# A two-layer hybrid trunk on one core: x, B and C of the scan fetched two chunks sooner, and the order of products and scalings in the output projections changed

## The chip, the core and the metric

The kernel runs on one core of one Trainium2 chip. The core has a matmul engine (TensorE, PE in the profile), VectorE (DVE), ScalarE (ACT), GpSimd (POOL) and SyncE (SP), which here only issues transfers. The metric is the device time of one execution in microseconds (us), lower is better. The profile is one execution, recorded by the hardware profiler; "L1555" in it is line 1555 of the kernel before.

## The reference, cut to what matters

```python
SEQ, D_MODEL, D_INNER = 1024, 1024, 2048          # one sequence, float32

def spatial_gating_mixer(h, w_in, ln_w, ln_b, w_s, b_s, w_out):          # layer 0
    z, u, v = split(h @ w_in, 3)                                         # 1024 -> 6144
    v = layernorm(v)                                                     # in 8 chunks of 128 tokens, 8 groups of 256
    mixed = einsum('gts,bcsgd->bctgd', tril(w_s), v) + b_s
    return (u * mixed * silu(z)) @ w_out                                 # 2048 -> 1024

def ssd_mixer(h, ...):                                                   # layer 1 (Mamba-2)
    z, xbc, dt = split(h @ w_in)                                         # 2048 | 4096 | 32 heads
    xbc = silu(causal_depthwise_conv(xbc, K=4));  x, B, C = split(xbc)
    dA_cs = cumsum(softplus(dt + bias) * A)                              # within a chunk of 128
    y = diag(C B^T * decay * dt) x + C (state before the chunk) * exp(dA_cs) + d_skip * x
    g = group_rmsnorm(y * silu(z), norm_w)                               # 8 groups of 256 channels
    return g @ w_out

h = x
for i in (0, 1): h = h + mixer_i(rmsnorm(h, norm_w[i]))
return rmsnorm(h, final_norm_w)
```

## The kernel before

**Matmuls in three.** Each float32 operand is split into a high part (a cast on ScalarE, L111) and a low part (a subtraction on VectorE, L112, or L742 where it is put off), and each product is three matmuls of 512 columns: high by high, high by low, low by high (`mm3`, L134 to L136). A name ending in h is a high part, in l a low part: `xh`, `xl` are those of a block of activations, `wh`, `wl` those of weights.

**Blocks.** The four large projections are computed as 2 x 2 block products with seven block products in place of eight (`Block` for the projections into a layer, `Out` for those out of it: `ao` for layer 0, `bo` for layer 1). In `Out`, A(i, j, c) is quarter c of block (i, j) of the activations (tiles `ya`), and B(k, l, c) that of the weights (tiles `wb`). `product(n)` runs one block product in four quarters; a quarter is 24 matmuls into four PSUM tiles `o[0]` to `o[3]` (four blocks of rows, two k each, three matmuls each). `prep(n, c)` splits the operands of a quarter, one quarter ahead. The order is 1, 7, 2, 6, 4, 5, 3 in `ao` and 1, 2, 7, 6, 4, 5, 3 in `bo`. Product 7 multiplies A(0, 0) + A(1, 0): the sum is made in place, for the first quarters on VectorE (`plus`, L762) and for the others as a DMA that adds (`add`, L759, on GpSimd's queue). In layer 1 each A quarter is loaded from DRAM (`g_d`, written by the scan) and scaled by the group norm's factors (L1766) when `ready` is called; `hook_b(n, c)` says at which quarter of which product the loads, scalings and sums of `bo` are issued. The factors come over DRAM: sums of squares to `ss_d`, back as `sv`, a power on GpSimd, `rs_d`, and back as `rb`.

**The scan.** Layer 1's scan goes over 64 chunks (8 groups of heads x 8 chunks of 128 tokens), n = 8g + c. Groups 0, 1, 3 and 5 are "spilt": their x, B and C after the convolution lie in DRAM (`xbc_d`) and come back 1 MB (four chunks) at a time by `prefetch(g, th, 0)` (L1555, tile `xbc`); `prefetch(g, th, 1)` loads z and the decay factors (`ze`). For the other groups the projection itself is computed during the scan (matmuls into `ab`, called by `project` as a filler between the scan's own matmuls), and its convolution and SiLU (tiles `x`, `bc`) are put into a queue that `drain` empties step by step. Each chunk loads 256 KB of decay inputs (`wl<-cs_d`, L1590) into one of four buffers, four chunks ahead, in pairs. At chunk n the transposes of chunk n + 3 (`pe_a`, L1595 and L1596, into `tp`), the weights (L1619), the diagonal product (`yy`, L1630), the states (`os`) and the gate follow one another. M = 50 is the chunk at which the projections end and product 1 of `bo` becomes the filler.

**The seam.** The last projection block before the scan runs its seven products in the order 1, 2, 6, 5, 7, 4, 3, one unit each. During it a last part of the activations (`f01`, L1378, tile `f`) is loaded again and split (`hh`, `hl`; `rest_a21`), and the last convolutions (`xc`) are put out.

**What sets the order.** The program order of each engine is the order of the calls; nothing reorders them. Tiles come from pools (16 buffers of 1 MB for `ya`, `wb`, `xbc`, `f`; four for `wl` of the scan; four for `xh` and `xl`), and an instruction that writes a tile waits for the last readers of the buffer's former tile. Transfers wait in the queue of the engine that issues them, and a transfer that waits holds up those behind it.

Of the kernel before, what the change touches and what calls it, by code (L numbers as in the profile page):

```python
# [15 lines left out]
P = 128  # L16
# [13 lines left out]
def kernel(  # L30
# [21 lines left out]
    nc = tc.nc  # L52
    x = x[0]
    out = out[0]
# [607 lines left out]
    class Out:  # L662
# [11 lines left out]
        def __init__(self, src, w, scale, res, accs, keep, order):  # L674
            self.src, self.w, self.scale, self.res, self.accs, self.keep = src, w, scale, res, accs, keep
            self.order, self.had, self.late, self.raw = order, set(), [], {}
            self.A, self.B, self.ops, self.acc, self.u, self.ss, self.guess = {}, {}, {}, {}, {}, {}, {}
            self.Y3, self.negs = [], []

        def half(self, th, nb):  # L680

# [110 lines left out]
        def product(self, n, hook=None):  # L792

            if n in (1, 2, 5):
                self.acc[n] = self.accs(n)
            if n == 4:
                t = s8([P, 4, 512], "u")
                self.u["c21"] = [t[:, k, :] for k in range(4)]
                for i in range(4):
                    nc.sync.dma_start(out=t[:, i, :], in_=self.res(4 + i, 0))  # L800
            o = self.acc[n] = self.acc[{7: 1, 6: 1, 4: 1, 3: 5}.get(n, n)]
            more = n not in (1, 2, 5)
            seq = [(m, c) for m in self.order[:6] for c in range(4)]
            now = n != 2 or self.order[1] == 7
            rest = []

            def low():
                while rest:
                    rest.pop(0)()

            for c in range(4):
                self.prep(n, c)
                at = seq.index((n, c)) + 1
                if at < len(seq) and not (n == 1 and c < 2 and self.scale is not None):
                    self.prep(*seq[at], rest)
                self.flush()
                if n == 1:
                    low()
                if hook is not None:
                    hook(n, c)  # L820
                low()
                X, Y = self.ops.pop((n, c))
                for i in range(4):
                    for k in range(2):
                        mm3(o[i], [m[:, k, i * P:(i + 1) * P] for m in X], [m[:, k, :] for m in Y],
                            not more and c == 0 and k == 0, c == 3 and k == 1, more)
                    if c == 3 and i and now:
                        self.post(n, i - 1)
                    if c == 3 and i == 3 and now:
                        self.post(n, i)  # L830
                    if n == (2 if self.order[1] == 7 else 6) and i == 0:
                        self.add(self.row(0, c, 0), self.res(c, 0))
                    if n == 4 and i == 3:
                        self.add(self.row(1, c, 1), self.res(4 + c, 1))
                    if n == 5 and i == 3:
                        self.add(self.row(0, c, 1), self.res(c, 1))
                    if i == 3:
                        for y in self.negs:
                            nc.scalar.mul(y, y, -1.0)
                        self.negs.clear()  # L840
                    yield
# [142 lines left out]
    late = []  # L984

    def finish():

        while late:
            late.pop(0)()
# [319 lines left out]
    xbc_d, todo = {}, []  # L1309
# [154 lines left out]
    def blocks():  # L1464


        ORDER, LAST = (1, 2, 6, 7, 5, 4, 3), (1, 2, 6, 5, 7, 4, 3)
        for g in SPILT:
            xbc_d[g] = dr.tile([P, 2, 4, 512], F32, name=f"xbc_d{g}")
        pairs = SPILT[:2], SPILT[2:]  # L1470
        bs = [zb[1], xbc_block("x", pairs[0]), zb[2], xbc_block("bc", pairs[0]), xbc_block("x", pairs[1]),
              xbc_block("bc", pairs[1]), zb[3]]
        bs[-1].apart = True
        seq = [(k, n) for k in range(len(bs)) for n in (ORDER if k < len(bs) - 1 else LAST)]
        small, turn, a21, done = decays(), [0], rest_a21(), []

        def ahead(at):
            if at < len(seq):
                k, n = seq[at]
                if n not in bs[k].Y:  # L1480
                    bs[k].prep(n)

        def unit(b, n, i):

            turn[0] += 1
            off = late[:]
            late.clear()
            if b is bs[-1]:
                if n in (1, 6):
                    late.append(todo.pop(0)())  # L1490
            elif done and todo and (turn[0] % 2 or len(todo) > 3):
                late.append(todo.pop(0)())
            b.mm(n, i, b is not bs[-1] or n != 5)
            if b is bs[-1] and n == 7:
                b.post(5, i)
                late.append(todo.pop(0)())
            for f in off:
                f()
            if not done and next(small, 0) == 0:
                done.append(True)  # L1500

        for at, (k, n) in enumerate(seq[1:], 1):
            b, nxt = bs[k], bs[k + 1] if k + 1 < len(bs) else None
            ahead(at + 1)
            if n == (2 if k else 7):
                b.fourth()
            if nxt is not None:
                if n == 1 or at == 1:
                    nxt.load(0, 1)
                if n == 6:  # L1510
                    nxt.load(0, 0)
                elif n == 5:
                    nxt.load(1, 0)
                    nxt.sums_b()
                elif n == 4:
                    nxt.load(1, 1)
            elif n == 6:
                next(pj)
            elif n == 5:
                next(a21)  # L1520
            elif n == 4:
                next(pj)
                next(a21)
            elif n == 3:
                next(pj)
                next(a21, None)
            for i in range(b.units):
                unit(b, n, i)
                if i == 0:
                    if nxt is not None and n == 7:  # L1530
                        nxt.sums_a()
                    ahead(at + 2)
        finish()

    with tc.manual_schedule():
# [245 lines left out]
    def hook_b(n, c):  # L1781
# [9 lines left out]
        elif at == (1, 3):  # L1791
            get("a", 0, 1, 2), get("b", 1, 0, 2)
            end["half"][0][1](), end["half"][0][2]()
            for k in (2, 3):
                get("a", 1, 0, k)
            bo.ready(1, 0, 0)
        elif n == 2:
            if c == 0:
                get("a", 0, 1, 3)
# [8 lines left out]
                bo.ready(1, 1, 0)  # L1808
            if c < 2:
                bo.b12_plus(1, c)  # L1810
            if c < 3:
                bo.ready(1, 0, c + 1)
            (bo.plus if c < 2 else bo.add)(bo.a(0, 0, c), bo.a(1, 0, c))
        elif n == 7:
            if c == 0:
                get("a", 1, 1, 3)
            if c < 2:
                bo.ready(1, 1, c + 1)
            if c < 3:
                bo.sums(2, c)  # L1820
        elif n == 6:
            if c == 0:
                bo.ready(1, 1, 3)
                bo.sums(2, 3)
            bo.sums(6, c)
            if c % 2 == 0:
                get("b12", 0, 1, c)
            if c == 0:
                end["fnwb"] = q4([P, D], "fnwb")
                nc.sync.dma_start(out=end["fnwb"], in_=final_norm_w.partition_broadcast(P))  # L1830
            elif c == 3:
                bo.b12_plus(0, 0)
            if c:
                bo.plus(bo.a(1, 0, c - 1), bo.a(1, 1, c - 1))
        elif n == 4:
            if c == 0:
                bo.plus(bo.a(1, 0, 3), bo.a(1, 1, 3))
                bo.b12_plus(0, 1)
            bo.post(2, c)
            if c % 2:  # L1840
                get("b", 1, 1, c - 1)
        elif n == 5:
            bo.prep_last(c)
            if c:
                weigh_left((c - 1) // 2, 2 * ((c - 1) % 2))
            if c == 3:
                bo.prep_unit(0)
# [13 lines left out]
    def scans():  # L1861
# [27 lines left out]
                    scan[g] = Scan(g, nc.gpsimd)  # L1889
                getattr(scan[g], f)(c, *a)  # L1890

        prefetch(0, 0, 0), prefetch(0, 0, 1)
        project(AHEAD // 2 + 1)
        while todo or late:
            convolve()
# [10 lines left out]
        at("decay", 2)  # L1906
        at("pe_a", 2), at("tokens", 2)
        for n, (g, c) in enumerate(chunks):
            if n == M + 3:
                drain(len(queue))  # L1910
            elif n == N - 9:
                for k in range(2):
                    bo.get("a", 0, 0, k)
            elif n == N - 7:
                end["scan"] = scan[G - 1]
                bo.get("b", 0, 0, 0)
# [60 lines left out]
                rs[g - 1][1]()  # L1977
            if c == 1 and g > 1:
                rs[g - 1][2]()
            k = n + 4  # L1980
            if c % 4 < 2 and k < N:
                prefetch(k // 8, k // 4 % 2, c % 4)
            project(want(n + 1))
        sc = scan[G - 1]
        for k in (0, 1):
# [67 lines left out]
```

## Time and profile before

| what | value |
|---|---|
| time, median of 3 runs (lowest to highest) | 1520.2 us (1519.4 to 1528.06) |
| the profiled execution: its time, its span | 1520.27 us, 1518.6 us |
| TensorE busy, mean granted clock | 1463.4 us (96%), 0.992 |
| VectorE, ScalarE, GpSimd busy | 1049.1, 784.2, 402.0 us (69%, 52%, 26%) |
| matmuls of `ao`: first to last | 530.3 to 690.6 us |
| the scan: first transpose, first and last diagonal product | 1007.3, 1019.0, 1353.7 us |
| matmuls of `bo`: first to last | 1339.1 to 1508.3 us |

A span runs from the first to the last instruction; 1.7 us of the execution's time lie around it. In rows of waits stand the engine, the tile that it wanted to write, the line, then what it waited for, and the total in us, the times and the longest. In rows of the timeline stand start and length in us, the engine ("SPq" is SyncE's queue of transfers), the line, the operation, out<-in, and in square brackets the idle time before it and what ended that. "PEclk" is the clock that TensorE was granted, as a share of full speed. Numbers of buffers are left out of names.

### The profile page before, as it was taken

How to read it: one execution, taken by the hardware profiler on the slowest of the kernel's cores; microseconds unless marked ns; L12 is line 12 of the kernel's file. 1: busy time of each engine (PE TensorE's matmuls, PEld its weight loads, DVE VectorE, ACT ScalarE, POOL GpSimd, SP SyncE). 2: the span in 40 equal slices, each digit the busy share in tenths (PEclk: the TensorE clock that was granted, in tenths of full speed). 3: DMA queues.
4: the chain of work that ended last, by engine and by line, in shares of the span. 5: the costliest groups of instructions: out<-in, count | busy, mean ns of one | idle time of the engine just before them, and what ended most of it. 6: DMA issues, size and time to landing. Idle time of an engine off the chain costs nothing. (4 is left out here: it accounts for less than half of the span.)

```text
span 1518.6 us, 21342 instructions
## 1 busy us (share of the span) xinstructions
PE 1463.4 (96%) x7834; PEld 1230.3 (81%) x7834; DVE 1049.1 (69%) x1713; ACT 784.2 (52%) x1256; POOL 402.0 (26%) x451
## 2 busy tenths in 40 slices
PE   6899999999999999999999999998999989999997
PEld 6899988888888888877878888877787878777875
DVE  7966566676666655678657467766677767688876
ACT  6533332232322445556666566565766676756463
POOL 1111110000000023202131313126666676642221
PEclk9999999999999999999999999999999999999999
DMA  5554323322322999948377888776656555589972
GB/s 183 140 169 143 106 89 108 110 105 101 116 87 79 361 247 243 257 133 163 112 174 161 182 169 162 153 235 188 180 145 191 166 181 140 159 264 276 250 162 111
DMA packets 174952, 254.45 MB, mean 168 GB/s; under 512 B 16400, under 2 KB 103168, under 8 KB 171648
## 3 DMA queue, kind: packets, MB, share of 16 engines
q1 hardware_dynamic: 124768, 168.93, 36.0%
q0 software_dynamic: 42448, 70.27, 23.0%
q10 hardware_dynamic: 7632, 13.90, 2.5%
q8 instruction: 62, 1.02, 0.3%
q14 instruction: 42, 0.34, 0.1%
HBM read 186.14 MB, written 51.18 MB: 156 GB/s over the span
## 5 line engine op out<-in xcount | busy, mean ns | idle before, releaser
L134 PE MATMUL acc<-hh,wh 128*128 128x512 f32 x868 | 340.1, 392 | 0.8 <-ACT u L296 0.8
L136 PE MATMUL acc<-hh,wl 128*128 128x512 f32 x868 | 338.5, 390 | 1.9 <-DVE wl L112 1.8
L135 PE MATMUL acc<-hl,wh 128*128 128x512 f32 x868 | 337.8, 389 | 0.0
L112 DVE TENSOR_TENSOR wl<-wr,wh 128x1024 fp32r<-128x1024 f32 (+1 forms) x96 | 114.3, 1192 | 118.7 <-ACT wh L111 118.6
L136 PEld LDWEIGHTS acc<-hh,wl 128*128 128x128 f32 x868 | 162.9, 188 | 37.8 <-DVE wl L112 3.6
L134 PEld LDWEIGHTS acc<-hh,wh 128*128 128x128 f32 x868 | 163.1, 188 | 35.0 <-ACT u L296 1.8
L135 PEld LDWEIGHTS acc<-hl,wh 128*128 128x128 f32 x868 | 163.0, 188 | 33.2
L296 ACT COPY u<-acc 128x512 f32<-128x512 f32 x115 | 66.9, 583 | 197.8 <-PE acc L136 197.7
L111 ACT CAST wh<-wr 128x1024 fp32r<-128x1024 f32 (+1 forms) x112 | 115.2, 1029 | 94.1 <-PE acc L135 56.6
L136 PE MATMUL acc<-wh,hl 128*128 128x256 f32 x448 | 129.2, 288 | 4.4 <-DVE hl L407 4.0
L134 PE MATMUL acc<-wh,hh 128*128 128x256 f32 x448 | 129.6, 289 | 2.4 <-DVE wh L418 1.0
L135 PE MATMUL acc<-wl,hh 128*128 128x256 f32 x448 | 128.6, 287 | 1.3 <-DVE wl L421 1.3
L134 PE MATMUL ab<-hh,wh 128*128 128x512 f32 x288 | 125.0, 434 | 0.8 <-DVE zt L999 0.8
L136 PE MATMUL ab<-hh,wl 128*128 128x512 f32 x288 | 114.2, 397 | 0.0
L135 PE MATMUL ab<-hl,wh 128*128 128x512 f32 x288 | 113.4, 394 | 0.0
L136 PEld LDWEIGHTS acc<-wh,hl 128*128 128x128 f32 x448 | 87.6, 196 | 5.6 <-DVE hl L407 4.7
L134 PEld LDWEIGHTS acc<-wh,hh 128*128 128x128 f32 x448 | 87.7, 196 | 3.4 <-ACT hh L400 1.4
L135 PEld LDWEIGHTS acc<-wl,hh 128*128 128x128 f32 x448 | 87.7, 196 | 1.7 <-DVE wl L421 1.5
L1601 ACT ACTIVATE wl<-wl,tk 128x128 f32<-128x128 f32 x256 | 81.6, 391 | 4.9 <-DMA wl<-cs_d 4.5
L649 POOL DMA_DIRECT2D y_d<-y x8 | 4.4, 549 | 290.6 <-DVE y L646 290.6
L135 PE MATMUL bo<-wl,xh 128*128 128x512 f32 x192 | 75.8, 395 | 5.4 <-DVE wl L112 2.4
L112 DVE TENSOR_TENSOR wl<-t,wh 128x1024 fp32r<-128x1024 f32 (+1 forms) x38 | 45.5, 1196 | 48.3 <-ACT wh L111 48.2
(314 smaller groups left out, 3248.1 us busy)
## 6 DMA issues: line engine op xcount, KB each, us to landing
wr<-in_a_w_in_dram SPq DMA_DIRECT2D x48, 512.0 KB, 3.7
wl<-cs_d SPq DMA_DIRECT2D x64, 256.0 KB, 4.6
wr<-in_b_w_in_dram SPq DMA_DIRECT2D x30, 512.0 KB, 8.4
wb<-in_a_w_out_dram SPq DMA_DIRECT2D x10, 1024.0 KB, 11.8
wb<-in_b_w_out_dram SPq DMA_DIRECT2D x10, 1024.0 KB, 8.9
wr<-in_b_w_in_dram SPq DMA_DIRECT2D x36, 256.0 KB, 6.0
v<-v_d SPq DMA_DIRECT2D x8, 1024.0 KB, 4.7
y_d<-y POOLq DMA_DIRECT2D x8, 1024.0 KB, 5.7
```

The costliest lines, as they stand in the source:

```text
L111: nc.scalar.copy(out=hi, in_=src)
L112: return (eng or nc.vector).tensor_tensor(out=lo, in0=src, in1=hi.bitcast(F32), op=ALU.subtract)
L134: nc.tensor.matmul(out=o, lhsT=l[0], rhs=r[0], start=start, stop=False, **kw)
L135: nc.tensor.matmul(out=o, lhsT=l[0], rhs=r[1], start=False, stop=False, **kw)
L136: nc.tensor.matmul(out=o, lhsT=l[1], rhs=r[0], start=False, stop=stop, **kw)
L296: nc.scalar.copy(out=self.u[n][:, i], in_=a)
L649: store = lambda: nc.gpsimd.dma_start(out=y_d[-1], in_=y)
L1601: nc.scalar.activation(wl[:, j, :], wl[:, j, :], AF.Relu, scale=-1.0, bias=tokc(2, c, self.g)[:, j:j + 1])
```

## The change

1. *Scan.* `prefetch` of part 0 (the 1 MB of x, B and C) is called two chunks sooner, and the first two of them ahead of everything. The last `drain` of the convolution queue is called at chunk M + 2 in place of M + 3.
2. *Seam.* `f01` is loaded at product 6 and not 5, ahead of two weight loads; both its splits follow product 4's unit; the last convolution is put out behind the loop; the operands of product 3 are prepared within product 7's unit.
3. *Products 1, 2 and 7 of both output projections.* In a quarter the eight high by high matmuls come first, over all four PSUM tiles, then the eight with `xl`, then the eight with `wl`. In the last quarter of products 1 and 2 the low ones go tile by tile; the last quarter of product 7 keeps the order of before.
4. *`bo`.* The scalings of A(1, 0, c), which product 7 wants, are issued a quarter later, behind the splits of the quarter (`after`), and so are the sums A(0, 0, c) + A(1, 0, c).

```diff
@@ Out.product
+                while self.after:
+                    self.after.pop(0)()
                 X, Y = self.ops.pop((n, c))
+                def mms(o=o, X=X, Y=Y, c=c, last=n in (1, 2, 7)):
+                    every = [(i, k) for i in range(4) for k in range(2)]
+                    if last and c < 3:
+                        seq3 = [(x_, y_, i, k) for x_, y_ in ((0, 0), (1, 0), (0, 1)) for i, k in every]
+                    elif last and n in (1, 2):
+                        seq3 = [(0, 0, i, k) for i, k in every] + \
+                            [(x_, 1 - x_, i, k) for i in range(4) for x_ in (1, 0) for k in range(2)]
+                    else:
+                        seq3 = [(x_, y_, i, k) for i, k in every for x_, y_ in ((0, 0), (0, 1), (1, 0))]
+                    for x_, y_, i, k in seq3:
+                        nc.tensor.matmul(out=o[i], lhsT=X[x_][:, k, i * P:(i + 1) * P], rhs=Y[y_][:, k, :],
...
+                todo = mms()
                 for i in range(4):
-                    for k in range(2):
-                        mm3(o[i], [m[:, k, i * P:(i + 1) * P] for m in X], [m[:, k, :] for m in Y],
-                            not more and c == 0 and k == 0, c == 3 and k == 1, more)
+                    for _ in range((12, 4, 4, 4)[i] if c == 3 and n in (1, 2) else 6):
+                        next(todo)
@@ blocks: unit(), and the loop over the last block's products
             if b is bs[-1] and n == 7:
                 b.post(5, i)
-                late.append(todo.pop(0)())
+                ahead(at + 2)
...
             elif n == 6:
+                next(a21)
                 next(pj)
-            elif n == 5:
-                next(a21)
             elif n == 4:
                 next(pj)
-                next(a21)
             elif n == 3:
                 next(pj)
-                next(a21, None)
             for i in range(b.units):
...
+                if nxt is None and n == 4:
+                    next(a21)
+                if nxt is None and n == 4:
+                    next(a21, None)
+        late.append(todo.pop(0)())
         finish()
@@ hook_b
                 get("a", 1, 0, k)
-            bo.ready(1, 0, 0)
         elif n == 2:
...
-            if c < 3:
-                bo.ready(1, 0, c + 1)
-            (bo.plus if c < 2 else bo.add)(bo.a(0, 0, c), bo.a(1, 0, c))
+            bo.after.append(lambda: bo.ready(1, 0, c))
+            if c:
+                (bo.plus if c < 3 else bo.add)(bo.a(0, 0, c - 1), bo.a(1, 0, c - 1))
         elif n == 7:
             if c == 0:
                 get("a", 1, 1, 3)
+                bo.add(bo.a(0, 0, 3), bo.a(1, 0, 3))
@@ the scan
-        prefetch(0, 0, 0), prefetch(0, 0, 1)
+        prefetch(0, 0, 0), prefetch(0, 0, 1), prefetch(0, 1, 0)
...
-            if n == M + 3:
+            if n == M + 2:
                 drain(len(queue))
...
+            k = n + 6
+            if k % 4 == 0 and k < N:
+                prefetch(k // 8, k // 4 % 2, 0)
             k = n + 4
-            if c % 4 < 2 and k < N:
-                prefetch(k // 8, k // 4 % 2, c % 4)
+            if c % 4 == 1 and k < N:
+                prefetch(k // 8, k // 4 % 2, 1)
```

SyncE's queue in the scan, around the load of the second half of group 1 (`xbc_d_6210`; `g_d` and `ss_d` are results and sums of the group before, `wr` weights of the filler), first before, then changed:

```order
L1704 DMA g_d_8254<-ze 256x1x512
L1559 DMA ze<-z_d_5288 128x2x512
L1563 DMA ze<-ecs_d 64x512 x4
L120 DMA wr<-in_b_w_in_dram 128x4x128 x2
L1590 DMA wl<-cs_d 128x512 x4
L1720 DMA ss_d<-gsq 2x256
L1555 DMA xbc<-xbc_d_6210 128x2048
```

```order
L1723 DMA g_d_8256<-ze 256x1x512
L1578 DMA ze<-z_d_5288 128x2x512
L1582 DMA ze<-ecs_d 64x512 x4
L120 DMA wr<-in_b_w_in_dram 128x4x128 x2
L1609 DMA wl<-cs_d 128x512 x2
L1574 DMA xbc<-xbc_d_6210 128x2048
L1609 DMA wl<-cs_d 128x512 x2
L1739 DMA ss_d<-gsq 2x256
```

The 1 MB load has moved from behind both pairs of decay inputs, and behind the sums, to between the two pairs.

VectorE during product 2 of `bo` (L1766, in the changed kernel L1785, is a scaling, L762 a sum, L742 and L112 the low parts; `sv` are the last group's sums of squares), before and changed:

```order
L1766 SCALAR_TENSOR_TENSOR ya<-ya,par,rb 128x512 x6
L762 TENSOR_TENSOR ya<-ya 128x1024
L742 TENSOR_TENSOR xl<-ya,xh 128x1024
L742 TENSOR_TENSOR wl<-wb,wh 128x1024
L1766 SCALAR_TENSOR_TENSOR ya<-ya,par,rb 128x512 x4
L762 TENSOR_TENSOR ya<-ya 128x1024
L742 TENSOR_TENSOR xl<-ya,xh 128x1024
L742 TENSOR_TENSOR wl<-wb,wh 128x1024
L1766 SCALAR_TENSOR_TENSOR ya<-x,par,rb 128x512 x2
L1732 TENSOR_SCALAR sv<-sv 128x4
L1766 SCALAR_TENSOR_TENSOR ya<-ya,par,rb 128x512 x2
L742 TENSOR_TENSOR xl<-ya,xh 128x1024
```

```order
L742 TENSOR_TENSOR wl<-wb,wh 128x1024
L1785 SCALAR_TENSOR_TENSOR ya<-ya,par,rb 128x512 x4
L762 TENSOR_TENSOR ya<-ya 128x1024
L742 TENSOR_TENSOR xl<-ya,xh 128x1024
L742 TENSOR_TENSOR wl<-wb,wh 128x1024
L1785 SCALAR_TENSOR_TENSOR ya<-ya,par,rb 128x512 x2
L1785 SCALAR_TENSOR_TENSOR ya<-x,par,rb 128x512 x2
L1751 TENSOR_SCALAR sv<-sv 128x4
L762 TENSOR_TENSOR ya<-ya 128x1024
L742 TENSOR_TENSOR xl<-ya,xh 128x1024
L742 TENSOR_TENSOR wl<-wb,wh 128x1024
L1785 SCALAR_TENSOR_TENSOR ya<-ya,par,rb 128x512 x2
```

One scaling pair of each quarter has gone from ahead of the quarter's low parts to behind them; in the last quarter of product 2 a sum stands ahead of `xl` instead.

GpSimd's queue at the turn from product 2 to product 7 (L141 is the power of the group norm; ya<-ya are the sums for product 7's third and fourth quarter, wb<-wb sums of weights for product 6), before and changed:

```order
L716 DMA wb<-in_b_w_out_dram 128x4x512 x2
L141 TENSOR_TENSOR rr<-sv,mhalf 128x4
L759 DMA ya<-ya 128x1024
L759 DMA wb<-wb 128x1024
L759 DMA ya<-ya 128x1024
L759 DMA wb<-wb 128x1024 x3
```

```order
L141 TENSOR_TENSOR rr<-sv,mhalf 128x4
L759 DMA wb<-wb 128x1024
L759 DMA ya<-ya 128x1024
L759 DMA wb<-wb 128x1024
L759 DMA ya<-ya 128x1024
L759 DMA wb<-wb 128x1024 x2
```

Each of the two ya sums has moved behind one more wb sum.

More of the change, by code (lines that the diff above doesn't have):

```diff
@@ L677, in __init__ @@
             self.A, self.B, self.ops, self.acc, self.u, self.ss, self.guess = {}, {}, {}, {}, {}, {}, {}
-            self.Y3, self.negs = [], []
+            self.Y3, self.negs, self.after = [], [], []
         def half(self, th, nb):
@@ L821, in product @@
                 low()
+                while self.after:
+                    self.after.pop(0)()
                 X, Y = self.ops.pop((n, c))
+                def mms(o=o, X=X, Y=Y, c=c, last=n in (1, 2, 7)):
[9 more added lines that the diff above has]
+                        nc.tensor.matmul(out=o[i], lhsT=X[x_][:, k, i * P:(i + 1) * P], rhs=Y[y_][:, k, :],
+                                         start=not more and c == 0 and k == 0 and x_ == y_,
+                                         stop=c == 3 and k == 1 and x_ != y_, skip_group_check=True)
+                        yield
+                todo = mms()
                 for i in range(4):
-                    for k in range(2):
-                        mm3(o[i], [m[:, k, i * P:(i + 1) * P] for m in X], [m[:, k, :] for m in Y],
-                            not more and c == 0 and k == 0, c == 3 and k == 1, more)
+                    for _ in range((12, 4, 4, 4)[i] if c == 3 and n in (1, 2) else 6):
+                        next(todo)
                     if c == 3 and i and now:
@@ L1481, in ahead, with unit @@
                     bs[k].prep(n)
-        def unit(b, n, i):
+        def unit(b, n, i, at=0):
             turn[0] += 1
@@ L1517, in blocks @@
             elif n == 6:
+                next(a21)
                 next(pj)
-            elif n == 5:
-                next(a21)
             elif n == 4:
                 next(pj)
-                next(a21)
             elif n == 3:
                 next(pj)
-                next(a21, None)
             for i in range(b.units):
-                unit(b, n, i)
+                unit(b, n, i, at)
                 if i == 0:
```

## The prediction

> **What bounds the kernel now.** I read the page's first two parts, then TensorE's waits, then the stretches in which those waits lie.
>
> ```profile
> PE 1463.4 (96%) x7834; PEld 1230.3 (81%) x7834; DVE 1049.1 (69%) x1713; ACT 784.2 (52%) x1256; POOL 402.0 (26%) x451
> PE   6899999999999999999999999998999989999997
> ```
>
> TensorE is busy for 96% of the span, so the kernel is bound by matmuls almost everywhere, and an edit that adds and drops no matmul can only win what TensorE idles or runs at a lower clock. The dips are at both ends, in slice 29 (the first part of the scan) and in slice 34 (where product 1 of the second out-projection gives way to product 2). TensorE's waits, longest in total first:
>
> ```profile
> PE tp L1595 <- DMA xbc<-xbc_d: 15.5, 7, 2.9
> ...
> PE bo L135 <- DVE wl L112: 2.4, 4, 1.0
> PE bo L135 <- DVE wl L742: 2.3, 3, 1.7
> PE acc L136 <- DVE wl L112: 1.8, 2, 1.3
> ...
> PE tp L1595 <- ACT bc L1433: 1.0, 1, 1.0
> ...
> PE ab L134 <- DVE zt L999: 0.8, 1, 0.8
> ```
>
> Columns: microseconds in total, times, longest. The first row is the scan: seven of the eight 1 MB loads of spilled x, B and C arrive after TensorE wants to transpose them. The others are the places that the change's other parts touch.
>
> **The scan's loads.** SyncE's queue around the fourth load, and TensorE at the same place:
>
> ```profile
> 1056.05 10.81 SPq L1590 DMA_DIRECT2D wl<-cs_d  x4
> 1067.59 0.34 SPq L1555 DMA_DIRECT2D xbc<-xbc_d  x1
> DMA to landing us min/median/max: 5.8/6.4/7.1
> 1074.79 0.87 PE L1595 MATMUL tp<-ident,xbc 128*128 128x128 f32 x3 [1.99 <-DMA xbc<-xbc_d]
> 1078.31 0.59 PE L1638 MATMUL os<-cw 128*128 128x256 f32 x2
> ```
>
> The load needs up to 7.1 us and is issued 1067.59, so it lands near 1074.7; TensorE had been ready 1.99 us before 1074.79. What delays the issue is the queue: four loads of decay inputs stand ahead, of which the second pair waits for the scan's own matmuls, so those four take from 1056.05 to 1066.9. In the changed order the load stands behind the first pair and ahead of the second, so it can go out near 1057, some 10 us sooner. The longest wait of all seven is 2.9 us; an advance of 10 covers it three times over. The slot that the load writes is one that an earlier chunk left: there is a new wait on its readers, and behind it on the queue stands the pair of decay loads; at the old place the load went out without any wait. I take **15.5 us** for this part; its ends are 0 (the load waits for its slot as late as before) and 15.5.
>
> Two of the waits also cost clock:
>
> ```profile
> core 0: us, PE busy (x) PEld busy (x) DVE busy (x) ACT busy (x) POOL busy (x), PEclk, DMA share, GB/s
> 1075.00:1078.00 3.00, 3.00 (x10) 2.53 (x10) 0.62 (x2) 2.97 (x8) 1.32 (x3) 0.50 1.05 232
> 1249.00:1252.00 3.00, 3.00 (x10) 2.47 (x9) 0.62 (x2) 1.57 (x4) 1.71 (x3) 0.50 0.31 93
> 1085.00:1130.00 45.00, 45.00 (x285) 37.30 (x283) 35.86 (x73) 31.14 (x67) 32.98 (x37) 1.00 0.54 146
> 1112.01 0.38 PE L1595 MATMUL tp<-ident,x 128*128 128x128 f32 x2
> 1113.72 0.39 PE L136 MATMUL ab<-hh,wl 128*128 128x512 f32 x1
> 1113.95 0.40 PE L134 MATMUL ab<-hh,wh 128*128 128x512 f32 x1
> ```
>
> The granted clock is 0.50 behind two of the seven waits. From 1074.79 to 1078.31 TensorE passes five transposes and six products in 3.52 us; the same eleven take 1.94 us at full clock (1112.01 to 1113.95). That is 1.58 us for each of two stretches, **3.2 us** together. They go with the waits; the lower end is 0, if short waits stay.
> By the Trainium skill ("TensorE: Matmul & The Clock Gate", section "HAM oscillation — how this bites in real kernels") only idle gaps above about 3.4 us bring the half rate. By that rule the half-clock stretches would have another cause than these waits of at most 2.9 us and would stay, and the sum would be 3.2 us smaller. The trace disagrees: the half rate begins at the end of such a wait, both times; and 1502.3 would still lie in the range of my forecast.
>
> Can the other engines follow without TensorE's pauses? The stretch 1085 to 1130 has no pause: TensorE is busy 45.00 of 45.00 us, and VectorE needs 35.86 of them, ScalarE 31.14, GpSimd 32.98. The cover is 9 us in 45, so I cost the faster pace at nothing; without it, VectorE would give back what it exceeds.
>
> **The seam into the scan.** SyncE's issue of f01, ScalarE's cast that waits for it, the cast of the first moved weight load, and TensorE's wait in the window 985 to 1060:
>
> ```profile
> 984.94 0.52 SPq L1378 DMA_DIRECT2D f<-f_d  x1
> 991.86 1.05 ACT L111 CAST hh<-f 128x1024 fp32r<-128x1024 f32 x1 [2.01 <-DMA f<-f_d]
> 994.90 1.05 ACT L111 CAST wh<-wr 128x1024 fp32r<-128x1024 f32 x1 [0.43 <-ACT xc L1353]
> PE acc L136 <- DVE wl L112: 1.3, 1, 1.3
> ```
>
> f01 moves ahead of two weight loads. Its slot comes free only when TensorE leaves an earlier product, so the two weight loads now stand behind that wait. They are first cast at 994.90, ten microseconds after f01's old issue, which hides a delay of the size of one load. The convolution taps that kept VectorE from the weight split (the 1.3) move behind the loop, and the early split of the last product's weights and of A21 takes away the 0.8 behind zt. At most 2.1 us go. But the moved convolution now runs later on ScalarE and VectorE, ahead of the first scan chunk. I take **1.0 us**, half of the rows, since one wait is replaced by a chain of the same engines; ends 2.1 and -1.0 (one cast of 1.05 late).
>
> **The last drain, one chunk sooner.** VectorE's last tap, ScalarE's table load and the SiLU:
>
> ```profile
> 1306.90 1.27 DVE L1322 SCALAR_TENSOR_TENSOR bc<-ab,par,bc 128x1021 f32<-128x1021 f32 x1
> 1307.90 1.28 ACT L1433 ACT_TABLE_LOAD   x1
> 1309.20 1.91 ACT L1433 ACTIVATE bc<-bc 128x2048 f32<-128x2048 f32 x1
> ```
>
> Two taps of 1.27 us and the SiLU with its 1.28 us table load go ahead of a chunk's weights and decay, so the SiLU begins some 4 us sooner and TensorE's wait of 1.0 us for it goes: **1.0 us**. What stands behind it on ScalarE comes 3.2 us (1.28 + 1.91) later, where TensorE shows no other wait in the scan; ends 1.0 and -1.0.
>
> **The second out-projection.** With the eight high by high matmuls first, a quarter wants xl only 8 x 0.23 = 1.8 us after its start and wl 3.6 us after it, where it wanted wl at the second matmul. The single waits are at most 1.7 us, so all 4.7 us of the two bo rows look covered. What is late next is read further on. First, waits that lie before the scan's end shift everything behind them (TensorE's waits in the window 1336 to 1366), and then the chain that ended last takes over:
>
> ```profile
> PE bo L135 <- DVE wl L112: 1.3, 2, 1.0
> PE bo L134 <- ACT wh L111: 0.3, 1, 0.3
> 1375.23 6.89 DMA ss_d<-gsq
> 1382.20 6.46 DMA sv<-ss_d
> 1391.71 1.31 POOL L759 DMA_DIRECT2D ya<-ya  x1
> 1409.96 1.06 ACT L111 CAST xh<-ya 128x1024 fp32r<-128x1024 f32 x1 [4.15 <-DMA ya<-ya]
> 1412.25 1.22 DVE L112 TENSOR_TENSOR wl<-wb,wh 128x1024 fp32r<-128x1024 f32 x1
> q0 software_dynamic: 548, 1.99, 100.7%
> ```
>
> 1.3 + 0.3 = 1.6 us are won for good. The rest, 3.1 us inside product 2, makes TensorE earlier against a chain that does not move: two transfers of 6.9 and 6.5 us bring the last group's sums at 1388.7, and from there go the scalings. Product 7's scalings are now a quarter later, and so is the sum for its last quarter, a DMA on GpSimd's queue. Before, it was issued at 1391.71 and its landing let the cast at 1409.96 begin, 18 us later. That queue was full: in 1401 to 1411 it took 100.7% of the DMA engines and moved 1.99 MB, 2.6 us for each 512 KB. In the changed order one wb sum goes ahead of both ya sums, and so the last ya sum lands one such place, 2.6 us, later. Its split ended at 1412.25 + 1.22 = 1413.5, and would end at 1416.1. The last quarter of product 7 keeps the old order and wants wl at its second matmul: in time of before, four quarters of 24 x 0.227 us behind 1392.5 (the same matmul of product 2's last quarter), at 1414.3. So 1.8 us of wait arise there, TensorE's lead is lost, and 1.6 - 1.8 is about nothing. I take **0.5 us**, since the queue may run a little ahead when the wb sum goes out sooner; ends 4.7 (all of both rows) and -3.0 (the sum, issued behind a scaling that is one quarter of 5.4 us later, lands that late: 1413.5 + 5.4 is 4.6 us past 1414.3, less 1.6).
>
> **The first out-projection** gets the same order. TensorE's whole list of waits from 500 to 720 is
>
> ```profile
> PE tp L1069 <- DVE nrm L1063: 0.5, 2, 0.3
> ```
>
> and none of it is a wait of its products' matmuls, so there is nothing to win. In the last quarter of products 1 and 2 the first result tile is now complete after twelve matmuls in place of six, 6 x 0.23 = 1.4 us later; its copy has the twelve matmuls that follow, 2.7 us, to hide behind, and without them it would cost 1.4 us. I take 0.
>
> **Sum.** 15.5 + 3.2 + 1.0 + 1.0 + 0.5 = 21.2 us. The durations are those of the profiled execution, which took 1520.27 us with a span of 1518.6; it stands at the median of the runs, 1520.2. 1520.3 - 21.2 = **1499.1 us**, 1.4% faster. A measurement of this kernel tells about 1% (15.2 us) from no change.
>
> **The rivals.**
> - The scan's loads stay partly late. For: the load is bound to a slot and to a queue whose head waits for matmuls. Against: the list above has ten microseconds of room. If half of 15.5 + 3.2 stays, the time is 1499.1 + 9.4 = 1508.5.
> - The decay inputs become late in place of x. Each 1 MB load now goes ahead of a pair of 256 KB loads and needs 6.4 us where the pair had been alone. For it speaks that ScalarE already waits for them, five times:
> ```profile
> ACT wl L1601: 4.5, 5
> ```
>  Against: none of these waits reaches TensorE. If each of eight pairs costs 0.9 us (4.5 / 5) there, that is 7.2: 1506.3.
> - Slower: the new order goes round four PSUM banks every two matmuls where the old one stayed in a bank for six. It touches 528 matmuls (three products of 96 in each of two layers, less the last quarter of product 7, twice). It decides from 21.2 us / 528 = 40 ns for each, that is from 0.27 us where a row above has 0.23 (1113.72 to 1113.95). At the half rate, 0.2 us more, it costs 106 us: 1605. Against it: 1085 to 1130 mixes four kinds of target tiles and stays at clock 1.00 and 45.00 of 45.00.
>  The Trainium skill (same page, section "A second HAM failure mode: psum-queue depth-cycling") describes a kernel that lost throughput by cycling through banks, with TensorE idling between groups and its clock swinging. By that rule this rival would be likely; the trace shows no swing where targets alternate.
> - The change does nothing in the out-projections and costs at the seam (both at their lower ends, -3.0 and -1.0): 18.7 + 1.0 - 4.0 gives 1504.6.
>
> **How the numbers follow.** The forecast, 1494 to 1503, has 0.69; late loads 0.08; late decay inputs 0.10; lower ends of seam and out-projection 0.09; the bank order, slower, 0.04. Low: all upper ends, 18.7 + 2.1 + 1.0 + 4.7 = 26.5, 1494. High: the late loads, 1509. Faster by over 1% means below 1505: the forecast, the lower ends, and a part of the decay rival, 0.80. Within 1%: 0.16. Slower: 0.04.
>
> **What would show it.** In the changed profile: no row of tp waiting for xbc among the first waits of TensorE, each xbc issue ahead of a pair of wl loads and near 10 us before its first transpose; no 0.50 clock in the scan; the row for bc gone; waits of bo for wl only in product 7, near its end, behind a ya sum, of 1 to 3 us; the matmuls of products 1, 2 and 7 still 0.23 us apart. I am wrong if TensorE's waits in the scan only change their name (to yy waiting for wl), or if the matmuls of the new order lie further apart.

## The result, and the profile after

The changed kernel takes 1502.27 us (median of 4 runs, 1499.79 to 1503.33) against 1521.36 us (4 runs, 1519.40 to 1528.06): a ratio of 0.9865 with a 95% interval of 0.9831 to 0.9898. The profiled execution took 1499.79 us, with a span of 1498.1; 1499.1 had been predicted for it. It is the lowest of the four; the median lies 0.7 us inside the end of the forecast, 1503.

The page after, its first row and TensorE's slices:

```profile
PE 1457.5 (97%) x7834; PEld 1227.5 (82%) x7834; DVE 1046.2 (70%) x1713; ACT 783.5 (52%) x1256; POOL 402.5 (27%) x451
PE   6899999999999999999999999999999999999997
```

Both dips have gone from the slices. TensorE's waits of the changed kernel, those of the projections into the layers left out:

```profile
engine line waited for: us in total, times, longest us
...
PE ab L134 <- ACT hh L111: 2.8, 1, 2.8
PE bo L835 <- ACT wh L111: 2.1, 2, 1.1
...
PE bo L835 <- DVE wl L112: 1.3, 2, 1.1
PE bo L835 <- DVE wl L1638: 1.1, 1, 1.1
...
PE bo L835 <- ACT wh L741: 0.4, 1, 0.4
```

No row of tp waiting for xbc or bc is left. But the seam waits longer than before (2.8 after 1.3 and 0.8), and the second out-projection (bo) still waits 5.8 us in all its rows, 2.5 of them now for high parts (wh), where it waited 5.9 before, 4.7 of them for low parts. The stretches of the scan, TensorE's busy time and granted clock (before, the first had 92.36 of 100 us and a clock of 0.98):

```profile
core 0: us, PE busy (x) PEld busy (x) DVE busy (x) ACT busy (x) POOL busy (x), PEclk, DMA share, GB/s
1020.00:1120.00 100.00, 100.00 (x634) 83.05 (x631) 74.67 (x157) 72.13 (x149) 70.92 (x81) 1.00 0.63 182
1120.00:1220.00 100.00, 100.00 (x642) 82.78 (x641) 75.05 (x161) 69.95 (x145) 71.22 (x80) 1.00 0.62 183
1220.00:1300.00 80.00, 80.00 (x517) 66.23 (x516) 57.38 (x131) 61.04 (x126) 60.27 (x68) 1.00 0.54 155
```

TensorE does not pause in 280 us, and the half clock went with the pauses. VectorE needs 75 of 100 us, so it follows.

Each run below is read by three stretches of its profile, since differences of 1 to 4 us are near the scatter of whole times: "in" is from the last matmul of `ao` to the first diagonal product of the scan (the projections into layer 1 and the seam), "scan" from there to the last diagonal product, "out" from there to the end of the span. All are in us, worked out from the starts of matmuls, from one profile of each kernel. The two profiles of the changed kernel (changed, e12) differ by 1.5 us in "in" and by nothing in the other two.

| kernel | in | scan | out | median (runs), ratio to before, interval |
|---|---|---|---|---|
| before | 328.2 | 334.7 | 164.9 | |
| changed | 329.1 | 313.0 | 165.6 | 1502.27 (4), 0.9865, 0.9831 to 0.9898 |
| e1: before + sooner loads | 327.8 | 315.0 | 164.3 | 1499.88 (4), 0.9842, 0.9824 to 0.9860 |
| e2: changed, loads as before | 329.3 | 334.0 | 169.1 | 1526.84 (10), 1.0026, 1.0008 to 1.0045 |
| e3: changed, scalings as before | 330.2 | 313.0 | 167.0 | 1503.16 (4), 0.9858, 0.9828 to 0.9888 |
| e4: changed, matmul order as before | 329.2 | 313.1 | 166.2 | 1501.95 (4), 0.9850, 0.9828 to 0.9872 |
| e5: changed, a weight load ahead of f01 | 325.5 | 313.0 | 168.0 | 1499.55 (4), 0.9846, 0.9815 to 0.9877 |
| e6: changed, ya sums on VectorE | 330.0 | 313.0 | 167.7 | 1504.02 (4), 0.9876, 0.9839 to 0.9913 |
| e7: changed, seam as before | 329.3 | 313.2 | 166.5 | 1502.03 (4), 0.9858, 0.9841 to 0.9875 |
| e8: changed, a scaling later | 328.3 | 313.0 | 166.3 | 1502.00 (4), 0.9859, 0.9833 to 0.9884 |
| e9: e5, e6 and e8 together | 325.2 | 313.0 | 163.6 | 1495.81 (4), 0.9818, 0.9792 to 0.9843 |
| e10: e9, matmul order as before | 324.9 | 313.1 | 165.1 | 1497.67 (4), 0.9834, 0.9817 to 0.9851 |
| e11: e9, product 7 high by high to its end | 325.9 | 313.2 | 163.5 | 1495.88 (5), 0.9822, 0.9805 to 0.9839 |
| e12: the changed kernel again | 330.5 | 313.0 | 165.6 | 1503.49 (4), 0.9874, 0.9856 to 0.9892 |

### The profile page after: what moved, and what is told of

The parts are those of the page before. It is cut to its first block, busy times and chain, and to the rows that moved or that the text cites. A ratio compares the mean times of both kernels' runs of the same rounds, so it can differ in the third digit from the quotient of the medians.

```text
span 1498.1 us, 21355 instructions
## 1 busy us (share of the span) xinstructions
PE 1457.5 (97%) x7834; PEld 1227.5 (82%) x7834; DVE 1046.2 (70%) x1713; ACT 783.5 (52%) x1256; POOL 402.5 (27%) x451
## 5 line engine op out<-in xcount | busy, mean ns | idle before, releaser
L112 DVE TENSOR_TENSOR wl<-wr,wh 128x1024 fp32r<-128x1024 f32 (+1 forms) x96 | 114.3, 1192 | 121.2 <-ACT wh L111 121.0
L112 DVE TENSOR_TENSOR wl<-t,wh 128x1024 fp32r<-128x1024 f32 (+1 forms) x38 | 45.4, 1196 | 47.0 <-ACT wh L111 46.9
L112 DVE TENSOR_TENSOR xl<-ya,xh 128x1024 fp32r<-128x1024 f32 x36 | 44.1, 1224 | 41.0 <-ACT xh L111 38.8
```

The costliest lines, as they stand in the source:

```text
L112: return (eng or nc.vector).tensor_tensor(out=lo, in0=src, in1=hi.bitcast(F32), op=ALU.subtract)
```

## The experiments

### The loads alone, and everything but the loads

e1 is the kernel before with this alone, and e2 takes it back out of the changed kernel:

```diff
-        prefetch(0, 0, 0), prefetch(0, 0, 1)
+        prefetch(0, 0, 0), prefetch(0, 0, 1), prefetch(0, 1, 0)
...
+            k = n + 6
+            if k % 4 == 0 and k < N:
+                prefetch(k // 8, k // 4 % 2, 0)
             k = n + 4
-            if c % 4 < 2 and k < N:
-                prefetch(k // 8, k // 4 % 2, c % 4)
+            if c % 4 == 1 and k < N:
+                prefetch(k // 8, k // 4 % 2, 1)
```

> The kernel before with the sooner loads of x, B and C alone (the last drain, the seam and the out-projections as before). If the loads carry the change, the seven waits of tp for xbc (15.5 us) and the two half-clock stretches (3.2 us) go and nothing takes their place: 18.7 us less than before, about 1501.5 us, with no row of tp waiting for xbc. If the pairs of decay inputs behind each 1 MB load become late in its place, waits of yy for wl come up and about 7 us are given back: 1508 us or more.

> The changed kernel with the loads of x, B and C where they were before. If the parts do not lean on each other, the 15.5 us of waits and about 3 us of half clock come back: 1518 us. If part of the scan's gain came from the drain, the seam or the matmul order, the time stays below 1513.

e1 takes 1499.88 us: the loads alone give all that the whole change gives. Its scan is 19.7 us shorter than before (334.7 to 315.0), where 18.7 were expected, and no wait of more than 0.3 us came in their place. Of its waits in layer 1 the longest are those that the kernel before has too, without the loads:

```profile
PE bo L135 <- DVE wl L112: 2.4, 4, 0.9
PE bo L135 <- DVE wl L742: 2.0, 2, 1.7
...
PE tp L1595 <- ACT bc L1433: 1.0, 1, 1.0
```

e2 has the waits back, and is slower than the kernel before, not 2 us faster:

```profile
PE tp L1614 <- DMA xbc<-xbc_d: 16.4, 7, 3.8
```

Its expectation missed by 9 us: 1526.84 where 1518 were due. Its "out" is 4.2 us longer than before and its "in" 1.1, so the parts other than the loads cost time by themselves in this run.

### Product 7's scalings, and the order of the matmuls

e3 issues the scalings and sums of product 7 as before; e4 has every quarter in the old order:

```diff
-            bo.after.append(lambda: bo.ready(1, 0, c))
-            if c:
-                (bo.plus if c < 3 else bo.add)(bo.a(0, 0, c - 1), bo.a(1, 0, c - 1))
+            if c < 3:
+                bo.ready(1, 0, c + 1)
+            (bo.plus if c < 2 else bo.add)(bo.a(0, 0, c), bo.a(1, 0, c))
```
```diff
-                def mms(o=o, X=X, Y=Y, c=c, last=n in (1, 2, 7)):
+                def mms(o=o, X=X, Y=Y, c=c, last=False):
```

> The changed kernel with product 7's scalings and the ya sums at the quarters where they were before; the high by high order stays. In the changed kernel product 7 waits 1.2, 1.2 and 1.3 us before its last three quarters' ends, behind ya sums that land on GpSimd's queue at 1383.3 and 1390.1. If the later sums cause this, they land some 3 us sooner here, product 7's waits fall from 3.7 to 1.5 us or less, and product 2 waits up to 1 us more: 1 to 2 us less than the changed kernel. If the load of A(1, 1, 2) (ya from g_d, landed 1388.8) binds product 7's last quarter anyway, its wait there stays above 1 us and the time is that of the changed kernel within 0.5 us.

> The changed kernel with every quarter of products 1, 2 and 7 in the old order (high by high, high by low, low by high for each tile), both layers; the scalings stay later. If going round four PSUM banks costs nothing, the matmuls of the first out-projection take as long as with the new order (160.5 us from first to last, within 0.3), and product 2 waits for wl again: 2 to 4 us more than the changed kernel, about 1503. If the bank order costs 10 ns for each of 528 matmuls, this kernel is 5 us faster in those products, half of it in the first out-projection (157.8 us).

Neither moves the time beyond its interval, and both expectations missed in size. In e3 the waits before the third and fourth quarter of product 7 went, as the sums' theory had it, but the last quarter waited 1.9 us for wl, with half clock behind it, and "out" is 1.4 us longer and not 1 to 2 shorter. All of that lies in product 2, which takes 24.6 us for the changed kernel's 23.1; product 7 takes 25.6 for 25.8. So something other than the sums holds its last quarter: VectorE waits 2.9 us there at the scaling for the load of A(1, 1, 2). In e4 "out" is only 0.6 us longer. `ao` took 161.9 us there and 160.5 both before and in the changed kernel. e4's extra is a wait of 0.8 us for wl and its restart, behind a cast that waited 3.5 us for its weight load (1.7 before, in the same order of matmuls; why that load was later is open), and no slower matmul: the bank order costs nothing. From start to start the matmuls of `ao` lie 227 ns apart in both orders (median). The mean matmul of the first out-projection, before and changed (mean ns behind the comma):

```profile
L134 PE MATMUL ao<-wh,xh 128*128 128x512 f32 x115 | 44.9, 391 | 0.0
```
```profile
L835 PE MATMUL ao<-wl,xh 128*128 128x512 f32 x115 | 33.5, 390 | 0.0
```

### What the seam and product 7 wait for

At the seam the changed kernel's timeline shows SyncE's queue and ScalarE's cast; the row behind it is the stretch after TensorE's wait, with the clock (0.65) third from its end:

```profile
980.12 0.34 SPq L1395 DMA_DIRECT2D f<-f_d  x1
980.58 10.63 SPq L120 DMA_DIRECT2D wr<-in_b_w_in_dram  x6
990.96 1.04 ACT L111 CAST wh<-wr 128x1024 fp32r<-128x1024 f32 x1 [4.00 <-DMA wr<-in_b_w_in_dram]
```
```profile
994.00:998.00 4.00, 3.98 (x12) 3.23 (x13) 3.98 (x4) 4.00 (x5) 0.56 (x1) 0.65 0.96 348
```

The weight load stands behind f01 and goes out at 980.6 (before, two weight loads went ahead of f01's 984.9). Its cast, now ahead of f01's casts in ScalarE's order, waits 4.0 us for it, TensorE waits 2.8, and a clock of 0.65 follows. In product 7, the timeline of GpSimd's sums, ScalarE's casts and VectorE, and then one row of the chain that ended last (start, length):

```profile
1371.64 0.84 POOL L759 DMA_DIRECT2D ya<-ya  x1 [2.04 <-DVE ya L1785]
1378.06 0.84 POOL L759 DMA_DIRECT2D ya<-ya  x1 [4.70 <-DVE ya L1785]
1383.41 1.05 ACT L111 CAST xh<-ya 128x1024 fp32r<-128x1024 f32 x1 [8.31 <-DMA ya<-ya]
1390.15 1.05 ACT L111 CAST xh<-ya 128x1024 fp32r<-128x1024 f32 x1 [4.75 <-DMA ya<-ya]
1388.90 1.42 DVE L1785 SCALAR_TENSOR_TENSOR ya<-ya,par,rb 128x512 f32<-128x512 f32 x2 [2.04 <-DMA ya<-g_d]
1392.50 1.22 DVE L112 TENSOR_TENSOR wl<-wb,wh 128x1024 fp32r<-128x1024 f32 x1
```
```profile
1363.59 25.22 DMA ya<-g_d
```

Both sums land 12 us after their issue and let a cast begin; and VectorE stands at a scaling whose load of 512 KB takes 25.2 us, with the low parts of the last quarter behind it. Three edits take one cause each:

```diff
 # e5, in projections() and in blocks() at product 6
-        for kh in range(2):
-            load(0, kh)
+        load(0, 0)
+        yield
+        load(0, 1)
...
             elif n == 6:
+                next(pj)
                 next(a21)
                 next(pj)
 # e6, in hook_b
-                (bo.plus if c < 3 else bo.add)(bo.a(0, 0, c - 1), bo.a(1, 0, c - 1))
+                bo.plus(bo.a(0, 0, c - 1), bo.a(1, 0, c - 1))
...
-                bo.add(bo.a(0, 0, 3), bo.a(1, 0, 3))
+                bo.plus(bo.a(0, 0, 3), bo.a(1, 0, 3))
 # e8, in hook_b at product 7
-            if c < 2:
-                bo.ready(1, 1, c + 1)
+            if c != 1 and c < 3:
+                bo.ready(1, 1, 1 if c == 0 else 2)
```

> The changed kernel with f01's load between the two weight loads that it had been put ahead of. In the changed kernel the cast of the first of them waits 4.0 us for its load, TensorE waits 2.8 us at the first product of the scan's filler and runs 2.5 us at half the clock behind it. If the weight load behind f01 causes this, the cast's wait goes, TensorE's wait falls below 1 us without half clock, and the first diagonal product of the scan comes 2 to 3 us sooner (1016.5 to 1017.5 instead of 1019.4): 1497 to 1498 in a profiled run. If the casts of f01 itself (hh, 993 to 995) bind the start, TensorE's wait stays above 2 us and the time is that of the changed kernel.

> The changed kernel with the two ya sums for product 7's last quarters on VectorE (two additions of 1.2 us) in place of GpSimd's queue. If their late landing on that queue is what product 7 waits for, the waits before its second, third and fourth quarter (1.2, 1.2, 1.3 us) fall to the last alone, which may stay because of the load of A(1, 1, 2) from g_d (landed 1388.8): 2 to 3 us less than the changed kernel from the scan's last diagonal product to the end (163.5 instead of 165.6). If that load binds, the waits move to the last quarter and the time does not change.

> The changed kernel with the scaling of A(1, 1, 2), which waits for its load from g_d, issued one quarter later, behind the low parts of product 7's last quarter. If VectorE standing at this scaling (2.0 us for the load that takes 25 us) makes the low parts late, the wait of 1.3 us in product 7's last quarter shrinks to below 0.5, while those of 1.2 us before the third and fourth quarter (for the ya sums) stay: about 1 us less. If the ya sums alone bind, nothing changes, since the cast of the last quarter's xh waits for the last sum until 1390.1 either way.

> The three edits together: f01 between the weight loads, both ya sums on VectorE, the scaling of A(1, 1, 2) a quarter later. If product 7's data and the weight load at the seam are what is left, both losses go: seam 2 to 3 us, product 7 3 to 4 us, together 5 to 7 us less than the changed kernel (about 1494 in a profiled run). If the chain over ss_d and sv, or VectorE itself, is the next bound, less than 3 us go.

e5 has no wait of TensorE at the seam and wins 3.6 us in "in" (325.5 for 329.1), more than the 2 to 3 expected; its "out" is 2.4 us longer, so most of it is lost again in product 7, and the whole time, 1499.55, is not clear of the changed kernel's. In e6 the two waits for the sums went, and the last quarter waited 4.0 us, in the wait's row and in VectorE's:

```profile
PE bo L835 <- DVE wl L112: 4.2, 2, 4.0
```
```profile
1391.98 1.41 DVE L1785 SCALAR_TENSOR_TENSOR ya<-ya,par,rb 128x512 f32<-128x512 f32 x2 [2.22 <-DMA ya<-g_d]
1395.58 1.22 DVE L112 TENSOR_TENSOR wl<-wb,wh 128x1024 fp32r<-128x1024 f32 x1
```

So the expectation's second case came, the load takes the sums' place, and it cost more than expected: half the clock followed the wait, and "out" is 2.1 us longer. e8 alone did not shorten "out" either (166.3), since there the casts still wait for the sums. With both edits, in e9, "out" is 163.6, 2.0 us shorter than the changed kernel's. e9 has e5's edit too, and no run has the two without it; e5's alone lengthened "out". With the seam mended e9 takes 1495.81 us. It beats both kernels: its interval ends at 0.9843, below e12's 0.9856 to 0.9892. Its longest waits in the second out-projection:

```profile
PE bo L835 <- DVE wl L1640: 1.1, 1, 1.1
PE bo L835 <- DVE stats L926: 0.6, 1, 0.6
PE bo L835 <- DVE u L897: 0.6, 1, 0.6
PE bo L835 <- DVE wl L112: 0.6, 2, 0.4
```

### The seam undone, and two variants of the mended kernel

e7 takes the seam's edits back (part 2 of the change). e10 and e11 start from e9: e10 with `last=False` as in e4, e11 with the last quarter of product 7 like those of products 1 and 2. e12 is the changed kernel, beside them on one chip.

> The changed kernel with the seam as it was before; the sooner loads, the last drain, the matmul order and the later scalings stay. If the seam's edits lose what they win, because the weight load behind f01 comes late, the first diagonal product stands 25.3 us behind the last matmul of the projections as before (28.6 in the changed kernel, whose last projection matmul is 2.9 us sooner), and the time is within 1 us of the changed kernel. If the seam won its 1.0 us as predicted, this kernel is 1 us slower.

> The kernel with the three mending edits (f01 between the weight loads, ya sums on VectorE, the scaling of A(1, 1, 2) a quarter later), with the old order of matmuls in products 1, 2 and 7 of both layers. If the high by high order is worth what the waits for wl say once product 7's data comes in time, product 2 waits for wl in its quarters again and the time from the scan's last diagonal product to the end grows by 2 to 4 us (from 163.6). If it is worth nothing, it grows by less than 0.5.

> The kernel with the three mending edits, and the last quarter of product 7 with its eight high by high matmuls first as well. There the kernel with three edits waits 0.5 us for wl and then 0.8 before product 6. If the old order in that quarter costs the first of these, 0.5 us less, too little for the times to show; the wait before product 6 (for an addition on VectorE) stays or grows.

> The changed kernel once more, beside the others on the same chip. If the three mending edits win 5 us or more, it stands that much above the run with the last quarter too: near 1501 against 1495 or 1496. If their gain was one chip's or one run's, the two lie within 2 us.

e7 takes 1502.03 us, 0.2 below the changed kernel's first median and 1.5 below e12's on the same chip, so the seam as it was before is no slower, and by the second pair even a little faster than the first of its two cases had it. Its first diagonal product is 25.5 us behind the last projection matmul (28.6 in the changed kernel and in e12). "In" is 328.4 us on average over the three profiles with the old seam (before, e1, e7) and 329.5 over the seven with the new one (changed, e2, e3, e4, e6, e8, e12): the seam's edits cost about 1.1 us, with a scatter of 1.5 (327.8 to 329.3) and 2.2 (328.3 to 330.5) in the two groups. With the weight load ahead of f01 (e5, e9, e10, e11) "in" is 324.9 to 325.9, some 3 us below the old seam. e10 shows what the high by high order is worth once product 7's data is in time: 1.5 us in "out" (165.1 against 163.6), less than the 2 to 4 expected; its `ao` is 1.6 us longer as well, with the same late weight load as in e4. e11 changes nothing, as expected; the wait before product 6 grew to 1.3 us. e12 against e11: 1503.49 and 1495.88 on the same chip, 7.6 us, so the mending is not one run's.

e12's own trace shows that what holds the second out-projection is not the same in every execution of one kernel. Its product 7 has no wait at its quarters (22.2 us, 25.8 in the first profile), but its product 2 takes 26.5 us for 23.1: the last quarter waits 2.5 us, with half clock behind it, for the cast behind a scaling that waits for the group norm's factors (`rb`):

```profile
PE bo L835 <- ACT wh L741: 2.5, 1, 2.5
1369.25 1.42 DVE L1785 SCALAR_TENSOR_TENSOR ya<-x,par,rb 128x512 f32<-128x512 f32 x2 [1.94 <-DMA rb<-rs_d]
1370.76 1.05 ACT L741 CAST xh<-ya 128x1024 fp32r<-128x1024 f32 x1 [3.45 <-DVE ya L1785]
```

So the factors that come over DRAM are a third holder. "Out" is 165.6 in both profiles, though the waits lie in different places. Why the factors came later in e12 was not tried.

## Why the prediction was right

**The scan's loads** were the change. Predicted: 18.7 us, by an issue between the pairs of decay inputs and near 10 us sooner. SyncE's queue around the fourth load, and its first transpose:

```profile
1050.39 1.00 SPq L1609 DMA_DIRECT2D wl<-cs_d  x2
1051.83 0.32 SPq L1574 DMA_DIRECT2D xbc<-xbc_d  x1
1059.13 0.80 SPq L1609 DMA_DIRECT2D wl<-cs_d  x2
1066.94 0.49 PE L1614 MATMUL tp<-ident,xbc 128*128 128x128 f32 x3
```

It goes out 15.1 us before TensorE takes it up; in the kernel before it went out 5.2 us before TensorE was ready for it, so it is 9.9 us sooner, and the new wait for its slot costs nothing. Measured in e1: 19.7 us, 1.0 more than the rows of waits and half clock; where that lies is open. The half clock's 3.2 us went with the waits, as summed. By the rule of the Trainium skill cited in the prediction ("TensorE: Matmul & The Clock Gate", section "HAM oscillation — how this bites in real kernels") it would have stayed; the clock of 1.00 in all three stretches of the scan decides against it for waits of this length, and in e2 it is back behind a wait of 2.5 us (1141.76).

**The last drain** was priced at the one wait that it removes, 1.0 us, and that wait is gone. Its size was not measured by itself: no run has the drain alone. All kernels with the sooner loads and the drain have a scan of 313.0 to 313.2, e1 without the drain 315.0. In that 2.0 us lies also what was won in product 1 ahead of the last diagonal product, where the prediction had put 1.6 (rows at 1339 to 1351 of the kernel before). So 2.0 stand for 2.6; the changed kernel still waits 1.1 us there, in one wait.

**The seam** is the step that failed. Predicted +1.0, measured -0.9 between the two profiles and -1.1 on average. The step was "ten microseconds after f01's old issue, which hides a delay of the size of one load": the slack of the weight loads was taken against the place of their cast before (994.90), but the change puts that cast ahead of f01's casts, where it would have begun at 987.0. It then waited 4.0 us (e5 removes it). Half clock behind the wait had no term.

**The second out-projection**: predicted +0.5, that is 1.6 ahead of the last diagonal product (in the stretch "scan", above) and -1.1 behind it; measured behind it -0.7 (164.9 to 165.6). The mechanism held: product 2's waits shrink (23.1 us for 25.0), and the lead is lost in product 7 (25.8 for 21.8) at data that does not come sooner. Its place was too narrow. The wait was put down to the last sum and the last quarter; the first trace has waits in three places, for both sums, and the runs found two more holders that the prediction did not see: the load of A(1, 1, 2) (before, VectorE waited 1.4 us there too), and in e12 the factors `rb`.

**The rivals.** Decay inputs did not become late: no wait of yy for wl in the changed kernel (one of 0.2 us in e1, for VectorE), and ScalarE's waits for them went only from 4.5 to 5.0 us. The bank order costs nothing, 391 and 390 ns a matmul. Of the two lower ends the seam's nearly came (-0.9 for -1.0); the out-projection's did not, it would have been -4.6 behind the last diagonal product. The sum came out at 20.5 us for 21.2 by errors of both signs: the loads 1.0 too small, the drain and product 1 together 0.6 too large, the rest of the out-projection 0.4 too low, the seam 1.9 too large, and 0.4 lie ahead of these stretches. The mechanism of the main term was right; that the total is so near is in part luck.

What stays open is why the load from g_d takes longer in one kernel than in another. e5's "out" is 2.4 us longer than the changed kernel's, and e2's 3.5 (4.2 to the kernel before). Of these 2.2 and 2.7 lie in product 7's last quarter, where the wait for wl is 1.7 and 2.1 us for 1.1, and half clock follows, which the changed kernel does not have there. VectorE waits there for the load from g_d, which takes 25.9 and 26.9 us for 25.2.

## What to carry to other kernels

Where a load stands in an in-order queue behind transfers that wait for compute, move its issue ahead of these, and price it by the wait's rows plus the clock lost behind them: that part was worth all of the gain here. A lead won on the busiest engine lasts only up to the next datum with a date of its own, so follow the operands of the next stages to their transfers before counting it, and look for more than one holder, in more than one profile: here two edits that won nothing alone came with 2 us less in a kernel that has both. Slack must be read at the place where the changed program reads the datum, not where the old one did.

## What the runs showed of the hardware

A load of 512 KB on SyncE's queue takes 25.2 us (1363.59 to 1388.81 in the changed kernel) while GpSimd's queue takes 80.4% of the DMA engines' time; SyncE's queue moves 2.36 MB in that stretch, so some 1.8 MB of other transfers on its own queue went in the same time. The 1 MB loads of the scan before land in 5.8 to 7.1. In the changed kernel the accumulating transfers of 512 KB on GpSimd's queue around product 7 land 2.5 to 3.8 us apart and 11.5 to 15.9 us after their issue, so that a sum of 1.2 us on VectorE is the quicker one.

The half clock comes on a grid. Apart from the beginning and the end of the kernel, each stretch at a granted clock of 0.50 lasts 3.41 us, and where a trace has several, their starts lie whole multiples of 3.413 us apart:

| kernel | starts of the half clock, us | steps of 3.413 us between them |
|---|---|---|
| before | 1074.72, 1248.80 | 51 |
| e2 | 994.98, 1141.76, 1250.98, 1418.23 | 43, 32, 49 |
| e3 | 997.12, 1396.48 | 117 |
| e12 | 997.93, 1373.40 | 110 |

The length of a wait alone does not decide: in e5 a wait of 1.66 us, which lies within one step, was followed by half the clock; in e2 one of 2.99 us (to 1054.51), which the grid parts into 1.49 and 1.50, was not. So the same wait can cost clock in one execution and none in the next; at the seam 2.8 us did in the changed kernel, and 2.7 in e8 did not. What else decides was not tried.
